# The decay of a gated linear recurrence: from tanh and reciprocal to an exponential on ScalarE

## The chip, the core and the metric

The kernel runs on one core of a Trainium2 chip. A core has TensorE (PE, matrix products; its weight loads are listed as PEld), VectorE (DVE), ScalarE (ACT), GpSimd (POOL) and SyncE (SP), whose queue issues most DMAs. Each engine runs its instructions in the order in which the program wrote them and waits on semaphores for others. The metric is device time in microseconds (us) of one execution, the median of the runs.

## What is computed

One layer of a streaming encoder over 2048 positions of width 1024: a mixer with three parallel branches (A a gated MLP over blocks, B a gated linear recurrence, C a state-space layer), then a two-level mixture of experts, then a norm. The change lies in branch B:

```python
def mixer_rglru(x_raw, g_raw, conv_w, conv_b, rg_w, rg_b, ig_w, ig_b, lam):
    xc = causal_depthwise_conv(x_raw, conv_w, conv_b)
    ...
    r = jax.nn.sigmoid(jnp.einsum("bshi,hij->bshj", xh, rg_w).reshape(bsz, seq, width) + rg_b)
    i = jax.nn.sigmoid(jnp.einsum("bshi,hij->bshj", xh, ig_w).reshape(bsz, seq, width) + ig_b)
    log_a = -LRU_C * r * jax.nn.softplus(-lam)          # LRU_C = 8
    a = jnp.exp(log_a)
    b = jnp.sqrt(-jnp.expm1(2.0 * log_a)) * (i * xc)
    h = linear_recurrence(a, b)                         # h_t = a_t * h_{t-1} + b_t
    return h * jax.nn.gelu(g_raw)
```

## The kernel before, in words

The mixer takes the sequence in two halves of 1024 positions. For each half the input projection `z = x @ W_in` runs in column chunks on TensorE (lines 90 to 92, three matmuls of a split product), and what follows a chunk is a Python generator, put into a list (`Flow`). Each `tick` of that list, called between the matmuls, lets every generator write its instructions up to its next `yield`; `yield 0` hands over within the same tick. A table `TURNS`, keyed by the generator's number and its step, moves single steps. So the order in which each engine gets its instructions is fixed by the steps of all generators, and a generator with a step less stands differently against the others.

Branch B has 12 tiles: two halves, three blocks of 128 channels, two quarters of 512 positions. `b_z` writes the projection of a tile, `b_post` the rest. In `b_post`: the convolution on `xc` (ScalarE line 906, then six VectorE instructions, line 171 as a helper's line, and a copy, line 912); the GELU of the gate (`bgg`, line 916); two gate matmuls (line 922) into two banks of the pool `psm`, which has two; their tanh (line 923) into `tr` (`btr` in the profile) and `ti` (`bti`); then the part that is changed; then the scan (line 939), the product with the gate on GpSimd (`bgg`), a DMA of it, its square (line 946) and a matmul against ones (line 950).

The part that is changed uses T = tanh(-log_a / 2): since a = 2/(1+T) - 1 and sqrt(1 - a^2) = 2 sqrt(T)/(1+T), it takes a tanh and a square root on ScalarE and a reciprocal on VectorE. `b_cols[:, :, 0]` holds the factor of that tanh, made once in `s5_consts`.

`s5_consts` is the setup of branch C; it runs between the tiles 1 to 4 of branch B, in rounds: in each, `angles` builds a table of sines on VectorE, ScalarE and GpSimd, and `outer` (line 691) products on VectorE and GpSimd; a matmul (line 734) into a `psm` bank is read by VectorE into `kp` (line 735), from where a DMA takes it. Later VectorE copies a weight of branch A out of PSUM (`wsT`, line 750). Lines 169, 170 and 171 are the helpers `tt`, `ts` and `stt`, so their instructions are told apart by their tiles. Line 212 and 216 scale the projection's weights on ScalarE; `c_batch` (lines 784 to 829) is branch C's batch with its own matmuls (792, 798, 817 to 819); `part` (lines 997 to 1015) is branch A's.

Of the kernel before, what the change touches and what calls it, by code (L numbers as in the profile page):

```python
# [9 lines left out]
F32 = mybir.dt.float32  # L10
# [3 lines left out]
AF = mybir.ActivationFunctionType  # L14
OP = mybir.AluOpType
# [4 lines left out]
P = 128  # L20
# [124 lines left out]
def phases12(tc, io, hd, hc, tab, gcol, ident, c8, stg):  # L145
# [3 lines left out]
    V, A, G, T = nc.vector, nc.scalar, nc.gpsimd, nc.tensor  # L149
    ctx = ExitStack()  # L150
    with ctx:
# [17 lines left out]
        tt = lambda o, a, b, op, e=V: e.tensor_tensor(out=o, in0=a, in1=b, op=op)  # L169
        ts = lambda o, a, s1, s2, o0, o1=OP.bypass, e=V: e.tensor_scalar(out=o, in0=a, scalar1=s1, scalar2=s2, op0=o0, op1=o1)  # L170
        stt = lambda o, a, s, b, o0, o1: V.scalar_tensor_tensor(out=o, in0=a, scalar=s, in1=b, op0=o0, op1=o1)  # L171
# [215 lines left out]
        b_cols = base.tile([P, 3, 4], F32, name="b_cols")  # L387
# [7 lines left out]
        def s5_consts(pp):  # L395
# [223 lines left out]
            t1, t2, t3 = sm("t1", 3), sm("t2", 3), sm("t3", 3)  # L619
# [21 lines left out]
            tt(t3, t3, t1, OP.add, e=G)  # L641
            yield 0
            ts(sp, t3, 2.0, None, OP.mult)
            yield 0
            ts(b_cols[:, :, 1], col("b_rg_b", 0, 3), 0.5, None, OP.mult)
            pass
# [237 lines left out]
        def b_z(h, i, w, q):  # L884
            N = 512
            F.until(lambda: all(("x", h * 8 + q * 4 + t) in done for t in range(4)) and "bcols" in done)
            st = {}
            for s in range(2):
                ps = bank(psz, "z")
                for k in range(8):  # L890
                    split3(nc, ps, [w[:, j, k, s * P:(s + 1) * P] for j in range(2)],
                           [xT[:, j, k, q * N:(q + 1) * N] for j in range(2)], k == 0, k == 7)
                    if k == 3:
                        F.tick()
                if s == 0:
                    F.add(b_post(h, i, q, ps, st))
                else:
                    st["g"] = ps
                F.tick()

        def b_post(h, i, q, px, st):
            N = 512
            bw = pools["b"]
            cw = lambda k: col("b_conv_w", k * 3 + i)
            xc = bw.tile([P, N], F32, name="bxc", bufs=2)
            A.activation(xc, px, AF.Identity, scale=cw(3), bias=col("b_conv_b", i))
            cst = hst[:, i, 0:3]
            for k in range(3):
                n = 3 - k
                stt(xc[:, n:], px[:, :N - n], cw(k), xc[:, n:], OP.mult, OP.add)  # L910
                stt(xc[:, :n], cst[:, k:3], cw(k), xc[:, :n], OP.mult, OP.add)
            V.tensor_copy(cst, px[:, N - 3:])
            while "g" not in st:
                yield
            gg = bw.tile([P, N], F32, name="bgg", bufs=2)
            A.activation(gg, st["g"], AF.Gelu_apprx_tanh)
            yield
            tr = bw.tile([P, N], F32, name="btr")
            ti = bw.tile([P, N], F32, name="bti")
            for j, o in enumerate((tr, ti)):  # L920
                ps = bank(psm, "m")
                T.matmul(ps, bd[:, j, i, :], xc, start=True, stop=True)
                A.activation(o, ps, AF.Tanh, scale=0.5, bias=b_cols[:, i, 1 + j:2 + j])
            yield

            A.activation(tr, tr, AF.Tanh, scale=b_cols[:, i, 0:1], bias=b_cols[:, i, 0:1])
            stt(ti, ti, 1.0, xc, OP.add, OP.mult)
            sq = bw.tile([P, N], F32, name="bsq")
            A.activation(sq, tr, AF.Sqrt)
            yield  # L930
            ts(tr, tr, 1.0, None, OP.add)
            V.reciprocal(out=tr, in_=tr)  # L932
            yield 0
            tt(sq, sq, tr, OP.mult)
            yield 0
            tt(ti, ti, sq, OP.mult)
            yield 0
            ts(tr, tr, 2.0, -1.0, OP.mult, OP.add)
            V.tensor_tensor_scan(out=xc, data0=tr, data1=ti, initial=hst[:, i, 3:4], op0=OP.mult, op1=OP.add)
            V.tensor_copy(hst[:, i, 3:4], xc[:, N - 1:N])  # L940
            yield
            tt(gg, gg, xc, OP.mult, G)
            yield
            t0 = h * 8 + q * 4
            nc.sync.dma_start(out=yTd[t0:t0 + 4, :, 3 + i, :].rearrange("t p n -> p t n"), in_=gg.rearrange("p (t n) -> p t n", n=P))
            A.activation(xc, gg, AF.Square)
            yield
            ps = bank(psm, "m")
            for t in range(4):
                T.matmul(ps[:, t:t + 1], xc[:, t * P:(t + 1) * P], ones, start=True, stop=True)  # L950
            s_ = ssd[:, 1, t0:t0 + 4]
            tt(s_, s_, ps[:, 0:4], OP.add)
            done.add(("b", h, i, q))
# [427 lines left out]
        open_pool("prep")  # L1381
        F.add(xprep(2))
        F.add(s5_consts(pools["prep"]))

        def pipeline(lst):
# [55 lines left out]
        for h in range(2):  # L1441
            F.until(lambda: ("r", h) in done)
            for m in range(4):
# [4 lines left out]
                for t in range(8):  # L1448
                    F.until(lambda: ("y", h * 8 + t) in done and h * 8 + t in ht)
                    N = 276 if m == 3 else 256  # L1450
# [551 lines left out]
```

## Time and profile before

| | |
|---|---|
| median of 3 runs | 1661.69 us (1660.15 to 1671.78) |
| the profiled execution | 1667.31 us, its span 1665.5 us |
| mean granted TensorE clock | 0.95 |
| TensorE busy | 1510.0 us, 91% of the span |
| VectorE busy | 1028.5 us, 62% |
| ScalarE busy | 915.6 us, 55% |
| GpSimd busy | 693.2 us, 42% |

The span runs from the first to the last instruction; 1.8 us of the execution lie around it. The profiled execution is 5.6 us above the median. Branch B's tiles stand between 95 and 555 us of the span; the experts' first matmul (line 1693) starts at 843.7 us.

### The profile page before, as it was taken

The page shows a single profiled execution, that of the slowest core. Times are in us where ns is not written, and L with a number is a line of the kernel's source. Part 1 is how long each engine was busy: PE and PEld are TensorE (multiplying, and loading weights), DVE is VectorE, ACT ScalarE, POOL GpSimd, SP SyncE. Part 2 cuts the span into 40 slices and gives each one's busy share as a digit, 9 for nine tenths or more (in the row PEclk, how much of TensorE's full clock was granted, in tenths as well). Part 3 has the DMA queues.
Part 4 walks back from the last instruction along what each step waited for, and adds up shares of the span by engine and source line. Part 5 has one row for each costly group of instructions (what it writes and reads, how often), then busy time and mean ns, then how long its engine had stood idle before and what let it go on. Part 6 is the DMA issues. An engine that isn't in the chain of part 4 may idle for free.

```text
span 1665.5 us, 25734 instructions
## 1 busy us (share of the span) xinstructions
PE 1510.0 (91%) x8389; PEld 1295.1 (78%) x8390; DVE 1028.5 (62%) x1813; ACT 915.6 (55%) x2029; POOL 693.2 (42%) x553
## 2 busy tenths in 40 slices
PE   7885689989999999989589969999999999999993
PEld 6763469966788999989578858888888888888882
DVE  6399876367365165777888877578788767403001
ACT  6455345656755556543144635666566656656662
POOL 1286412142202153442144534556555555545442
PEclk8998799999999999999789989999999999999996
DMA  6232572331262352940677878678978876633442
GB/s 165 70 71 60 95 208 78 114 102 51 77 209 64 134 202 77 339 155 37 220 256 228 247 239 243 172 196 261 280 228 244 251 223 195 176 83 96 86 115 79
DMA packets 210063, 267.47 MB, mean 161 GB/s; under 512 B 30600, under 2 KB 174160, under 8 KB 209936
## 3 DMA queue, kind: packets, MB, share of 16 engines
q1 hardware_dynamic: 185456, 203.52, 38.6%
q0 software_dynamic: 24480, 62.27, 15.5%
q8 instruction: 78, 1.28, 0.3%
q14 instruction: 49, 0.40, 0.1%
HBM read 217.09 MB, written 76.94 MB: 177 GB/s over the span
## 4 chain that ended last, share of the span: by engine, by line
PE 61%; DVE 14%; DMA 6%; ACT 3%; issue 2%; POOL 1%; SPq 1%; POOLq 0%; DVEq 0%; ACTq 0%
PE pg L1693 21%; PE z L90 6%; PE z L92 6%; PE z L91 6%; PE pd L1734 4%; PE pd L1733 4%; PE pd L1732 4%; DMA stg<-in_expert_w_up_dram 3%; DVE ring L1601 2%; DVE ring L1619 2%; PE pt L1700 2%; DVE btr L932 1%; PE pt L1705 1%; PE ph L1700 1%; PE m L246 1%
## 5 line engine op out<-in xcount | busy, mean ns | idle before, releaser
L1693 PE MATMUL pg<-ring,xs 128*128 x2016 | 488.2, 395 | 14.1 <-DVE ring L1619 13.0
L1693 PEld LDWEIGHTS pg<-ring,xs 128*128 128x128 f32 x2016 | 378.5, 190 | 94.3 <-issue 16.5
L90 PE MATMUL z<-w,xT 128*128 128x256 f32 (+1 forms) x848 | 252.3, 297 | 17.9 <-ACT xT L302 8.9
L169 POOL TENSOR_TENSOR w<-raw,w 128x512 fp32r<-128x512 f32 x84 | 115.0, 1371 | 348.3 <-ACT raw L216 302.9
L92 PE MATMUL z<-w,xT 128*128 128x256 f32 (+1 forms) x848 | 246.5, 291 | 5.8 <-DVE xT L169 5.7
L91 PE MATMUL z<-w,xT 128*128 128x256 f32 (+1 forms) x848 | 245.9, 290 | 0.0
L1601 DVE TENSOR_SCALAR ring<-stg,gcol 128x512 fp32r<-128x512 f32 x242 | 133.3, 612 | 166.4 <-PE pg L1693 86.7
L1619 DVE SCALAR_TENSOR_TENSOR ring<-stg,gcol,ring 128x512 fp32r<-128x512 f32 x248 | 218.4, 940 | 0.0
L90 PEld LDWEIGHTS z<-w,xT 128*128 128x128 f32 x848 | 166.1, 196 | 21.7 <-issue 10.4
L92 PEld LDWEIGHTS z<-w,xT 128*128 128x128 f32 x848 | 165.6, 195 | 7.2 <-DVE xT L169 7.2
L91 PEld LDWEIGHTS z<-w,xT 128*128 128x128 f32 x848 | 166.2, 196 | 1.7 <-issue 1.7
L1897 POOL DMA_INDIRECT hd<-yb,tab x41 | 75.8, 1848 | 180.5 <-ACT yb L1836 180.5
L1732 PE MATMUL pd<-ring,hh 128*128 x336 | 131.5, 391 | 1.7 <-DVE hh L1638 1.7
L1733 PE MATMUL pd<-ring,hh 128*128 x336 | 131.2, 390 | 0.0
L1734 PE MATMUL pd<-ring,hh 128*128 x336 | 131.2, 390 | 0.0
L1911 POOL TENSOR_TENSOR hs<-hs,hu 128x256 f32<-128x256 f32 x84 | 102.1, 1215 | 54.0 <-ACT hu L1815 51.5
L1946 POOL TENSOR_TENSOR yb<-yb,gf 128x1024 f32<-128x1024 f32 x40 | 117.0, 2924 | 6.8 <-ACT hu L1861 6.8
L171 DVE SCALAR_TENSOR_TENSOR ht<-z,rsd,ht 128x256 f32<-128x256 f32 x176 | 84.7, 483 | 49.8 <-PE z L92 40.3
L90 PE MATMUL z<-xT,w 128*128 128x512 f32 x256 | 113.4, 443 | 0.2 <-ACT xT L302 0.2
L212 ACT ACTIVATE w<-raw,vec 128x256 fp32r<-128x256 f32 x176 | 86.6, 495 | 48.1 <-PE z L92 47.2
L91 PE MATMUL z<-xT,w 128*128 128x512 f32 x256 | 103.6, 405 | 0.2 <-DVE xT L169 0.2
L92 PE MATMUL z<-xT,w 128*128 128x512 f32 x256 | 103.1, 403 | 0.0
(443 smaller groups left out, 2862.0 us busy)
## 6 DMA issues: line engine op xcount, KB each, us to landing
stg<-in_expert_w_gate_dram SPq DMA_DIRECT2D x62, 512.0 KB
stg<-in_expert_w_up_dram SPq DMA_DIRECT2D x62, 512.0 KB
stg<-in_expert_w_down_dram SPq DMA_DIRECT2D x60, 512.0 KB
raw<-in_w_in_dram SPq DMA_DIRECT2D x48, 256.0 KB
raw<-in_w_out_dram SPq DMA_DIRECT2D x24, 512.0 KB
ht<-in_x_dram SPq DMA_DIRECT2D x16, 512.0 KB
yp<-yTd SPq DMA_DIRECT2D x8, 1024.0 KB
hd<-ht SPq DMA_DIRECT2D x16, 512.0 KB
```

What stands on the lines that cost most here:

```text
L90: nc.tensor.matmul(ps, ah, bh, start=first, stop=False)
L91: nc.tensor.matmul(ps, ah, bl, start=False, stop=False)
L92: nc.tensor.matmul(ps, al, bh, start=False, stop=last)
L169: tt = lambda o, a, b, op, e=V: e.tensor_tensor(out=o, in0=a, in1=b, op=op)
L1601: x = v.tensor_scalar(out=ring[:, r, 0, sl], in0=src[:, sl], scalar1=g, scalar2=None, op0=OP.mult)
L1619: x = v.scalar_tensor_tensor(out=ring[:, r, 1, sl], in0=src[:, sl], scalar=g, in1=hi, op0=OP.mult, op1=OP.subtract)
L1693: i = t.matmul(pg[f], xx[j // 2], w[j % 2], start=k == 0 and j == 0, stop=k == 7 and j == 2)
L1732: t.matmul(pd[n], hh[:, 0, kf], w[0], start=kf == 0, stop=False)
L1733: t.matmul(pd[n], hh[:, 0, kf], w[1], start=False, stop=False)
L1734: i = t.matmul(pd[n], hh[:, 1, kf], w[0], start=False, stop=kf == 3)
L1911: g.tensor_tensor(out=o, in0=o, in1=hu[:, f * 256:(f + 1) * 256], op=OP.mult).then_inc(s_hm, 1)
L1946: g.tensor_tensor(out=z, in0=z, in1=gf, op=OP.mult).then_inc(p_z, 1)
```

## The change

The decay a is taken directly: its logarithm is log_a = -4 softplus(-lam) (1 + t), where t is the tanh of the gate that `tr` holds, so one `Exp` with a scale and a bias per channel gives it (`b_cols[:, :, 3]`, made once). T stays, for the square root: sqrt(1 - a^2) / 2 = (1 + a) sqrt(T/4). The reciprocal and the three VectorE instructions around it go; one instruction with two operations comes.

```diff
@@ s5_consts
             ts(sp, t3, 2.0, None, OP.mult)
+            ts(b_cols[:, :, 3], t3, -4.0, None, OP.mult)
             yield 0
@@ b_post
-            A.activation(tr, tr, AF.Tanh, scale=b_cols[:, i, 0:1], bias=b_cols[:, i, 0:1])
+            sq = bw.tile([P, N], F32, name="bsq")
+            A.activation(sq, tr, AF.Tanh, scale=b_cols[:, i, 0:1], bias=b_cols[:, i, 0:1])
             stt(ti, ti, 1.0, xc, OP.add, OP.mult)
-            sq = bw.tile([P, N], F32, name="bsq")
-            A.activation(sq, tr, AF.Sqrt)
-            yield
-            ts(tr, tr, 1.0, None, OP.add)
-            V.reciprocal(out=tr, in_=tr)
-            yield 0
-            tt(sq, sq, tr, OP.mult)
+            A.activation(tr, tr, AF.Exp, scale=b_cols[:, i, 3:4], bias=b_cols[:, i, 3:4])
+            A.activation(sq, sq, AF.Sqrt, scale=0.25)
+            yield
+            stt(sq, tr, 1.0, sq, OP.add, OP.mult)
             yield 0
             tt(ti, ti, sq, OP.mult)
             yield 0
-            ts(tr, tr, 2.0, -1.0, OP.mult, OP.add)
             V.tensor_tensor_scan(out=xc, data0=tr, data1=ti, initial=hst[:, i, 3:4], op0=OP.mult, op1=OP.add)
```

Behind the change the lines of `b_post` before the scan shift by up to two. VectorE's order in the first tile's changed part, from the copy that ends the second tile's convolution (`hst` keeps a tile's last values; a row is line, operation, output<-inputs and size; the scan of line 939 is listed as SCALAR_TENSOR_TENSOR), before:

```order
L912 COPY hst<-z 128x3
L170 TENSOR_SCALAR btr<-btr 128x512
L932 RECIPROCAL btr<-btr 128x512
L169 TENSOR_TENSOR bsq<-bsq,btr 128x512
L169 TENSOR_TENSOR bti<-bti,bsq 128x512
L170 TENSOR_SCALAR btr<-btr 128x512
L939 SCALAR_TENSOR_TENSOR bxc<-btr,hst,bti 128x512
L940 COPY hst<-bxc 128x1
L735 COPY kp<-tp 16x4x128
```

and with the change:

```order
L913 COPY hst<-z 128x3
L171 SCALAR_TENSOR_TENSOR bsq<-btr,bsq 128x512
L169 TENSOR_TENSOR bti<-bti,bsq 128x512
L937 SCALAR_TENSOR_TENSOR bxc<-btr,hst,bti 128x512
L938 COPY hst<-bxc 128x1
L736 COPY kp<-tp 16x4x128
```

Four instructions ahead of the scan have become one, and the copy `kp` stands right behind as before. ScalarE's order in the fourth tile, before:

```order
L793 ACTIVATE cx<-tp 128x256
L926 ACTIVATE btr<-btr,b_cols 128x512
L929 ACT_TABLE_LOAD
L929 ACTIVATE bsq<-btr 128x512
L906 ACTIVATE bxc<-z,vec 128x512
L212 ACTIVATE w<-raw,vec 128x256
```

and with the change:

```order
L794 ACTIVATE cx<-tp 128x256
L928 ACTIVATE bsq<-btr,b_cols 128x512
L930 ACT_TABLE_LOAD
L930 ACTIVATE btr<-btr,b_cols 128x512
L931 ACT_TABLE_LOAD
L931 ACTIVATE bsq<-bsq 128x512
L907 ACTIVATE bxc<-z,vec 128x512
L212 ACTIVATE w<-raw,vec 128x256
```

The exponential and a table load of its own stand between the tanh and the square root's load, and so ahead of the next tile's convolution `bxc`. This is so in all 12 tiles: 34 table loads become 46, and no load at another place comes or goes. ScalarE's order behind the seventh tile's square root, before:

```order
L916 ACT_TABLE_LOAD
L916 ACTIVATE bgg<-z 128x512
L946 ACTIVATE bxc<-bgg 128x512
L923 ACTIVATE btr<-m,b_cols 128x512
L923 ACTIVATE bti<-m,b_cols 128x512
L1011 ACTIVATE uv<-tp 128x4x128 x2
```

and with the change:

```order
L917 ACT_TABLE_LOAD
L917 ACTIVATE bgg<-z 128x512
L924 ACTIVATE btr<-m,b_cols 128x512
L924 ACTIVATE bti<-m,b_cols 128x512
L944 ACTIVATE bxc<-bgg 128x512
L1009 ACTIVATE uv<-tp 128x4x128 x2
```

The square of the gated output (946, now 944) has gone behind the two tanh of the eighth tile. Besides, in two places GpSimd's product `bgg` stands one or two of its weight products earlier, TensorE's matmul against ones (950) of one tile of the second half stands 52 instructions earlier, and VectorE's instructions of a tile stand closer together where others lay between them.

## Rows read from the trace of the kernel before

**Rows 1.** The page's part 1: busy time of each engine, its share of the span and its number of instructions.

```profile
PE 1510.0 (91%) x8389; PEld 1295.1 (78%) x8390; DVE 1028.5 (62%) x1813; ACT 915.6 (55%) x2029; POOL 693.2 (42%) x553
```

**Rows 2.** Busy time of each engine in five stretches of the first third (columns: the stretch in us, its length, busy us of PE, PEld, DVE, ACT and POOL with their instructions, granted TensorE clock, DMA share, GB/s).

```profile
100.00:203.00 103.00, 62.79 (x254) 43.58 (x253) 100.81 (x109) 46.67 (x72) 69.39 (x54) 0.82 0.41 84
203.00:240.00 37.00, 30.12 (x143) 23.43 (x142) 23.84 (x49) 16.45 (x30) 7.61 (x8) 0.87 0.67 169
240.00:340.00 100.00, 97.51 (x714) 90.40 (x713) 53.06 (x126) 58.31 (x136) 15.04 (x17) 0.97 0.39 124
340.00:430.00 90.00, 78.08 (x351) 59.66 (x350) 62.11 (x106) 61.63 (x139) 29.41 (x23) 0.95 0.24 71
430.00:560.00 130.00, 128.21 (x829) 113.48 (x828) 64.57 (x128) 73.44 (x158) 25.63 (x21) 0.97 0.38 116
```

**Rows 3.** The instructions on tiles `btr` and `bti`, over the whole span (line, engine, operation, names, count: shortest/median/longest ns, first and last start in us, form).

```profile
L170 DVE TENSOR_SCALAR btr<-btr x24: 414/419/1700, 133.0 to 536.3; 128x512 f32<-128x512 f32 x24
L926 ACT ACTIVATE btr<-btr,b_cols x12: 801/806/842, 115.2 to 525.4; 128x512 f32<-128x512 f32 x12
L929 ACT ACTIVATE bsq<-btr x12: 629/632/636, 117.3 to 527.5; 128x512 f32<-128x512 f32 x12
L932 DVE RECIPROCAL btr<-btr x12: 3353/3353/3355, 133.4 to 531.6; 128x512 f32<-128x512 f32 x12
L169 DVE TENSOR_TENSOR bsq<-bsq,btr x12: 679/692/753, 136.8 to 534.9; 128x512 f32<-128x512 f32 x12
...
L171 DVE SCALAR_TENSOR_TENSOR bti<-bti,bxc x12: 681/684/1577, 128.5 to 515.9; 128x512 f32<-128x512 f32 x12
```

**Rows 4.** The groups of ScalarE by shape: the table loads charged to line 929 (count, busy us, mean ns, idle us before them).

```profile
L929 ACT ACT_TABLE_LOAD x12 | 15.4, 1283 | 0.2
```

**Rows 5.** VectorE in order of time, three stretches (start us, us, engine, line, operation, names, form, count).

```profile
132.98 0.42 DVE L170 TENSOR_SCALAR btr<-btr 128x512 f32<-128x512 f32 x1
...
138.68 1.28 DVE L939 TENSOR_TENSOR_SCAN bxc<-btr,hst,bti 128x512 f32<-128x512 f32 x1
...
140.08 0.68 DVE L735 COPY kp<-tp 16x512 f32<-16x512 f32 x1
...
164.97 1.70 DVE L170 TENSOR_SCALAR btr<-btr 128x512 f32<-128x512 f32 x1
...
171.88 1.28 DVE L939 TENSOR_TENSOR_SCAN bxc<-btr,hst,bti 128x512 f32<-128x512 f32 x1
...
194.41 0.42 DVE L170 TENSOR_SCALAR btr<-btr 128x512 f32<-128x512 f32 x1
...
200.04 1.28 DVE L939 TENSOR_TENSOR_SCAN bxc<-btr,hst,bti 128x512 f32<-128x512 f32 x1
```

**Rows 6.** TensorE in order of time, the second gate matmul (L922) of the tiles 2, 3 and 4, with the idle time before it and what ended it in brackets.

```profile
140.81 2.08 PE L922 MATMUL m<-bxc,bd 128*128 128x512 f32 x2 [6.70 <-DVE kp L735]
...
174.02 2.08 PE L922 MATMUL m<-bxc,bd 128*128 128x512 f32 x2 [6.96 <-DVE kp L735]
...
202.17 2.08 PE L922 MATMUL m<-bxc,bd 128*128 128x512 f32 x2 [6.63 <-DVE kp L735]
```

**Rows 7.** ScalarE in order of time: the square root of the second tile.

```profile
147.52 0.64 ACT L929 ACTIVATE bsq<-btr 128x512 f32<-128x512 f32 x1
```

**Rows 8.** ScalarE and then VectorE in order of time around the fourth tile.

```profile
212.38 0.80 ACT L926 ACTIVATE btr<-btr,b_cols 128x512 f32<-128x512 f32 x1
...
215.03 0.76 ACT L906 ACTIVATE bxc<-z,vec 128x512 f32<-128x512 f32 x1
...
215.82 0.75 DVE L171 SCALAR_TENSOR_TENSOR bxc<-z,vec,bxc 128x509 f32<-128x509 f32 x1 [6.19 <-ACT bxc L906]
...
219.15 1.01 DVE L750 COPY wsT<-tp 128x384 f32<-128x384 f32 x2
```

**Rows 9.** TensorE in order of time: three of its gaps after the setup.

```profile
219.76 0.69 PE L792 MATMUL tp<-ident,zk 128*128 128x128 f32 x2 [0.81 <-DVE wsT L750]
...
232.48 1.12 PE L922 MATMUL m<-bxc,bd 128*128 128x512 f32 x2 [0.93 <-DVE cv L169]
...
287.01 1.05 PE L950 MATMUL m<-ones,bxc 128*128 128x1 f32 x8 [0.88 <-ACT raw L242]
```

**Rows 10.** ScalarE in order of time around 280 us.

```profile
279.64 0.38 ACT L967 ACTIVATE uv<-z 128x256 f32<-128x256 f32 x1 [3.87 <-DVE tab L170]
...
285.14 0.63 ACT L946 ACTIVATE bxc<-bgg 128x512 f32<-128x512 f32 x1 [0.85 <-POOL bgg L169]
```

**Rows 11.** TensorE in order of time, second half of the sequence: the gate matmuls of tile 9, and two gaps.

```profile
397.41 1.88 PE L922 MATMUL m<-bxc,bd 128*128 128x512 f32 x4
...
403.76 1.96 PE L997 MATMUL m<-uv,wsT 128*128 128x512 f32 x4 [1.68 <-ACT btr L923]
...
423.89 1.56 PE L239 MATMUL tp<-ident,raw 128*128 128x128 f32 x8 [2.06 <-ACT btr L923]
```

**Rows 12.** ScalarE in order of time in the same stretch.

```profile
402.93 0.69 ACT L923 ACTIVATE btr<-m,b_cols 128x512 f32<-128x512 f32 x1 [4.62 <-DVE bxc L939]
...
407.45 0.81 ACT L926 ACTIVATE btr<-btr,b_cols 128x512 f32<-128x512 f32 x1
...
423.15 0.68 ACT L923 ACTIVATE btr<-m,b_cols 128x512 f32<-128x512 f32 x1
```

**Rows 13.** TensorE in order of time: its last gap in the recurrent branch's stretch.

```profile
544.55 4.13 PE L879 MATMUL m<-ones,yc 128*128 128x1 f32 x30 [0.57 <-ACT yc L874]
```

## The prediction, made before the changed kernel ran

> **What bounds the kernel now.** I read the page's busy times first. TensorE is busy 91% of the span [rows 1], so a microsecond saved elsewhere is worth one only where TensorE waits for it. The second view is the table of stretches, read for the busy time of each engine against the length of the stretch. From 100 to 203 us VectorE is busy 100.8 of 103 us and TensorE 62.8: there VectorE is the bound. From 240 to 340 and from 430 to 560 us TensorE has 97.5 of 100 and 128.2 of 130. Between 340 and 430 us it has 78.1 of 90, and ScalarE and VectorE are both near 62 [rows 2]. The third view is TensorE in order of time with the reason for each gap. In the setup each round has a gap of 6.6 to 7.0 us in front of the second gate matmul, released by the copy `kp` on VectorE [rows 6]: that matmul needs the PSUM bank that `kp` empties, and `kp` stands in VectorE's queue behind the previous tile's reciprocal and scan [rows 5]. So the setup's end is a chain on VectorE through the changed instructions of tiles 1, 2 and 3.
>
> **What the change does to VectorE.** Per tile four instructions go: two `ts` of 0.42, the reciprocal of 3.35 and the product of 0.69 us, together 4.88. One `stt` comes; the nearest row is the same form on `bti`, 0.68 us at the median and 1.58 at the worst [rows 3]. Net 4.2 us less per tile (3.3 at worst), 50 us in 12 tiles.
>
> **What it does to ScalarE.** An `Exp` over 128x512 with a scale and a bias per channel is in no row. Below it lies the square root without such operands, 0.63, above it the longest tanh with them, 0.84; I take that tanh's median, 0.81, since shape and operands are the same [rows 3]. The added table load is 1.28 us with next to no idle time around it (0.2 us in all twelve) [rows 4]. Together 2.1 us per tile, 25 us in 12 tiles (1.9 to 2.15). One small instruction for `b_cols` in the setup counts as nothing against this.
>
> A rule of the Trainium skill speaks against this change. On the row, a load costs 1.28 us with no idle time to speak of [rows 4]. "ScalarE: Activation LUTs", section "What ACT_TABLE_LOAD costs", has 1283 ns for the load, which the trace confirms, and another 1380 ns of drain at every switch, which it does not show. By that price each tile would pay 3.5 us on ScalarE, and the sum below would be about 2.8 us smaller.
>
> **A, the setup: 13.0 us less.** From the first removed instruction to the start of the scan VectorE takes 138.68 - 132.98 = 5.70, 171.88 - 164.97 = 6.91 and 200.04 - 194.41 = 5.63 us [rows 5]. With the change 0.68 + 0.69 of work and small steps between remain, 1.48. That leaves 4.2, 5.4 and 4.15, or 13.8 in all; the second includes a `ts` that took 1.70 instead of 0.42, a stall that the new instruction may meet in its place, so 12.5 is the other end. I take 13.0. The longer ScalarE chain does not come into the way: tile 2's root starts at 147.52 and VectorE wants it at 164.97 [rows 5, 7], 17 us of cover against 2.1. What is late next after each saved piece is the rest of VectorE's round: it is busy 98% of the stretch, and GpSimd with 69.4 us and TensorE with 62.8 still fit into 90 [rows 2]. After the third round the DMAs that `kp` feeds, and behind them branch C, simply start earlier, and TensorE follows as a whole.
>
> **B, the fourth tile: 1.7 us more.** Here ScalarE's chain has no cover. Its tanh starts at 212.38, the next convolution's first step at 215.03, and VectorE, idle for 6.19 us, starts on that at 215.82. Behind the convolution it copies `wsT` at 219.15 [rows 8], and TensorE waits 0.81 us for that at 219.76 [rows 9]. With `Exp` and a load in between, all of this moves by 2.1 us, and TensorE has no slack to hide it. Queued behind are branch C's transposes and batches. Some of it comes back: at 232.48 TensorE waits 0.93 us for a bank that VectorE empties behind tile 4's scan; that chain is 4.2 shorter, so only the product itself remains of that wait, about 0.4 returns. Net +1.7 (0 to 2.1).
>
> **C, near 287 us: 0.9 less.** TensorE's 0.88 us wait [rows 9] is for a square on ScalarE at 285.14, behind GpSimd's product. That hangs on ScalarE's weight scaling, which stands behind an evacuation that waited 3.87 us for VectorE at 279.64, where tile 6's chain was in front of it [rows 10]. With 4.2 us less there it closes.
>
> **D, tiles 7 to 10: 2.6 less.** At 402.93 ScalarE has waited 4.62 us for tile 8's scan, and runs from there without a pause to 423.15, where TensorE waits for it (gaps of 1.68 and 2.06 us) [rows 11, 12]. With the change the scan is done before TensorE's gate matmuls, which begin at 397.41 and take 1.88 us; moved up by the 0.7 us that tile 7 gives back, they let ScalarE start at about 398.2, 4.7 us earlier. Inside the run lies tile 9's chain (its tanh at 407.45) with 2.1 us more. So ScalarE reaches the point at 423.15 some 2.6 us earlier, and TensorE with it. It still waits there: ScalarE keeps half of what VectorE gave. The swap of the square and the two tanh in tile 8 only helps here.
>
> **E, at 544 us: 0.6 less.** TensorE's last gap, 0.57 us [rows 13], is for a square behind products that VectorE begins after tile 12's scan; that ends 4 us earlier. The other tiles (5, 6, 11) lie beside a TensorE that is nearly always busy and count as nothing; what hides the 2.1 us there are projection results waiting in four PSUM banks. Without that cover each would cost at most 2.1. The moved `bgg` products and the earlier matmul against ones find their inputs ready, and count as nothing.
>
> **The sum** is -13.0 + 1.7 - 0.9 - 2.6 - 0.6 = -15.4 us. The experts behind 560 us keep their order and their durations, so they start earlier as a block. The profiled execution took 1667.3 us and would take 1651.9. It stands 5.6 us above the median, and nothing in it says where; the runs shown spread from 1660.15 to 1671.78. From the median of 1661.7 the forecast is **1646.3 us**.
>
> **Rivals.**
> 1. *More than that.* After gaps of 6.6 to 7.0 us TensorE starts slowly: two gate passes take 2.08 us [rows 6], where four take 1.88 at 397.41 [rows 11], and the granted clock is 0.82 and 0.87 in the first two stretches [rows 2], between the levels of 1.2 and 2.4 GHz. The gaps shrink to about 2.6, and the clock may stay up. In the setup that changes nothing, since VectorE is the bound; from 203 to 240 us 30.1 us of TensorE work at 0.87 could become 26.2, 3.9 less. With A at 13.8 the time is 1641.6. Against it: another wait for a DMA falls into that stretch.
> 2. *ScalarE pays more at a switch.* If each added switch costs its load's 1.28 us [rows 4] once again, in waiting, a tile has 3.4 us more in place of 2.1: B grows by 1.3, D shrinks by 1.3, and the time is 1648.9. The 0.2 us of idle time before twelve loads speak against it. The drain in the Trainium skill's "ScalarE: Activation LUTs" is such a cost.
> 3. *The setup does not shrink.* GpSimd works in step with VectorE there; if half of each saving turns into a wait for its products, A is 6.5 and the time 1652.8. GpSimd's 67% of that stretch [rows 2] speaks against it.
> 4. *Slower.* ScalarE's convolution step stands behind the new load in every tile, and VectorE and TensorE behind it, as in B. Were all 12 tiles like the fourth, without the gain of A, the price would be 12 x 2.1 = 25 us and the time 1686.8. It decides where ScalarE's chain has less than 2.1 us of cover; the setup's tiles have 17 [rows 5, 7].
> 5. *The change does not do what it says*: the order shows that all 12 reciprocals go, and that each tile gets one load more, no other; this I count at nothing.
>
> **How the numbers follow.** Forecast 0.60, rival 1 0.18, rival 2 0.08, rival 3 0.10, rival 4 0.04. One per cent, 16.6 us, is about what a measurement of this kernel can tell from no change: under 1645.1 is faster. The forecast's own spread, from the ends of A, B and `Exp`, is some 4 us to each side; a third of its chance lies below the line, 0.20, and rival 1 nearly whole, 0.17: faster 0.37. Slower is rival 4, 0.04. The rest, 0.59, is within 1%. The range for 8 in 10 goes from below rival 1 by half the forecast's own spread to above rival 3 by as much, since the median itself moves by a few microseconds: 1639 to 1655.
>
> **What would show it.** In the profile of the changed kernel: VectorE about 50 us less busy, ScalarE 25 more, 46 table loads; the gaps in front of `kp`'s matmul down from 6.6 to 7.0 us to 1.5 to 2.7; the third setup round's scan ending 13 us earlier, at about 188; TensorE's gap before the transpose near 207 (219.76 before) up from 0.8 to 2.9; a wait for ScalarE's gate tanh still there near 409. The forecast is wrong if the setup's rounds do not get shorter, or if TensorE shows new waits for ScalarE between 230 and 330 or behind 420 us.

## The result and the profile after

The changed kernel takes 1644.33 us (median of 4 runs, 1638.97 to 1648.28), the kernel before beside it 1662.65 us: a ratio of 0.988 (95% interval 0.983 to 0.993), 18.3 us less by the medians. The ratios here and below are not quotients of the two medians and can differ from them by up to 0.002. Repeated beside two other series it took 1643.49 (0.990, 0.988 to 0.993) and 1647.88 us (0.991, 0.989 to 0.993). The forecast was 1646.3. The profiled execution of the changed kernel took 1643.64 us, its span 1641.9.

Busy time of each engine, part 1 of the page of the changed kernel, to be held against [rows 1]:

```profile
PE 1508.7 (92%) x8389; PEld 1294.2 (79%) x8390; DVE 976.0 (59%) x1778; ACT 942.4 (57%) x2053; POOL 692.8 (42%) x553
```

VectorE has lost 52.5 us and ScalarE gained 26.8 (forecast 50 and 25); TensorE's work is the same. Of the 52.5 us the time got less than 20.

VectorE in the setup's three rounds, changed kernel, in order of time (the instruction that replaced the reciprocal, the scan, and in the first round the copy `kp`):

```profile
134.45 0.68 DVE L171 SCALAR_TENSOR_TENSOR bsq<-btr,bsq 128x512 f32<-128x512 f32 x1
...
135.96 1.28 DVE L937 TENSOR_TENSOR_SCAN bxc<-btr,hst,bti 128x512 f32<-128x512 f32 x1
...
137.36 0.68 DVE L736 COPY kp<-tp 16x512 f32<-16x512 f32 x1
...
162.28 1.97 DVE L171 SCALAR_TENSOR_TENSOR bsq<-btr,bsq 128x512 f32<-128x512 f32 x1
...
165.01 1.28 DVE L937 TENSOR_TENSOR_SCAN bxc<-btr,hst,bti 128x512 f32<-128x512 f32 x1
...
187.52 0.68 DVE L171 SCALAR_TENSOR_TENSOR bsq<-btr,bsq 128x512 f32<-128x512 f32 x1
...
188.96 1.28 DVE L937 TENSOR_TENSOR_SCAN bxc<-btr,hst,bti 128x512 f32<-128x512 f32 x1
```

From the first instruction of the changed part to the scan the three rounds took 5.70, 6.91 and 5.63 us [rows 5]; now 1.51, 2.73 and 1.44. That is 12.6 less in all.

TensorE's gaps in the changed kernel (idle time and its releaser in brackets), to be held against [rows 6, 9, 11]:

```profile
138.09 2.08 PE L923 MATMUL m<-bxc,bd 128*128 128x512 f32 x2 [1.56 <-DVE kp L736]
...
167.14 2.07 PE L923 MATMUL m<-bxc,bd 128*128 128x512 f32 x2 [2.78 <-DVE kp L736]
...
191.09 2.07 PE L923 MATMUL m<-bxc,bd 128*128 128x512 f32 x2 [1.52 <-DVE kp L736]
...
204.24 0.55 PE L750 MATMUL tp<-ident,big 128*128 128x128 f32 x3 [3.76 <-DMA big<-in_a_spatial_w_dram]
...
210.75 0.69 PE L793 MATMUL tp<-ident,zk 128*128 128x128 f32 x2 [2.32 <-DVE wsT L751]
...
249.83 1.10 PE L923 MATMUL m<-bxc,bd 128*128 128x512 f32 x2 [1.28 <-DVE cv L169]
...
409.14 1.72 PE L239 MATMUL tp<-ident,raw 128*128 128x128 f32 x8 [2.97 <-ACT btr L924]
...
473.65 1.16 PE L799 MATMUL m<-cx,cpp 128*128 128x128 f32 x8 [1.39 <-ACT raw L242]
```

In front of the matmul that waits for `kp` 6.6 to 7.0 us [rows 6] are down to 1.5 to 2.8 (1.5 to 3.3 in the two repeats). The gap for `wsT` is 2.32 where it was 0.81 [rows 9]; the other two gaps of [rows 9] are gone, as are the 1.68 us at 403.76 [rows 11] and the last one [rows 13]. A wait for ScalarE's gate tanh near 409 stays (2.97 for 2.06). One wait for VectorE, 1.28 us at 249.83 in front of tile 6's gate matmuls, and one for ScalarE, 1.39 us at 473.65, are new; a new wait for ScalarE behind 420 us is one of the signs by which the prediction was to be wrong.

ScalarE in the fourth tile, changed kernel (against [rows 8]), and the two groups of table loads of the changed part over the whole span:

```profile
201.27 0.80 ACT L928 ACTIVATE bsq<-btr,b_cols 128x512 f32<-128x512 f32 x1
202.09 1.28 ACT L930 ACT_TABLE_LOAD   x1
203.38 0.81 ACT L930 ACTIVATE btr<-btr,b_cols 128x512 f32<-128x512 f32 x1
204.20 1.28 ACT L931 ACT_TABLE_LOAD   x1
205.50 0.63 ACT L931 ACTIVATE bsq<-bsq 128x512 f32<-128x512 f32 x1
206.03 0.76 ACT L907 ACTIVATE bxc<-z,vec 128x512 f32<-128x512 f32 x1
```

```profile
L930 ACT ACT_TABLE_LOAD x12 | 15.4, 1283 | 0.2
L931 ACT ACT_TABLE_LOAD x12 | 15.4, 1283 | 0.1
```

From the tanh's start to the convolution's it is 4.76 us, where it was 215.03 - 212.38 = 2.65 [rows 8]: 2.11 more. Of that the exponential is 0.81 and the load 1.28, and what follows a load starts 0.01 to 0.02 us behind it.

### The profile page after: what moved, and what is told of

It reads as the page before. It is cut to its first block, busy times and chain, and to the rows that moved or that the text cites. A ratio compares the mean times of both kernels' runs of the same rounds, so it can differ in the third digit from the quotient of the medians.

```text
span 1641.9 us, 25729 instructions
## 1 busy us (share of the span) xinstructions
PE 1508.7 (92%) x8389; PEld 1294.2 (79%) x8390; DVE 976.0 (59%) x1778; ACT 942.4 (57%) x2053; POOL 692.8 (42%) x553
## 3 DMA queue, kind: packets, MB, share of 16 engines
q0 software_dynamic: 24480, 62.27, 15.6%
q8 instruction: 78, 1.28, 0.3%
## 4 chain that ended last, share of the span: by engine, by line
PE 64%; DVE 12%; DMA 5%; ACT 4%; issue 2%; POOL 1%; SPq 0%; POOLq 0%; DVEq 0%; ACTq 0%
PE pg L1691 22%; PE z L90 7%; PE z L91 6%; PE z L92 6%; PE pd L1732 4%; PE pd L1730 4%; PE pd L1731 4%; DMA stg<-in_expert_w_up_dram 3%; DVE ring L1599 2%; DVE ring L1617 2%; PE pt L1698 2%; PE pt L1703 1%; DVE bxc L171 1%; PE ph L1698 1%; PE m L863 1%
## 5 line engine op out<-in xcount | busy, mean ns | idle before, releaser
L1599 DVE TENSOR_SCALAR ring<-stg,gcol 128x512 fp32r<-128x512 f32 x242 | 143.8, 655 | 169.9 <-PE pg L1691 87.6
L1617 DVE SCALAR_TENSOR_TENSOR ring<-stg,gcol,ring 128x512 fp32r<-128x512 f32 x248 | 203.1, 879 | 0.0
```

The lines of the kernel that those rows point to most:

```text
L1599: x = v.tensor_scalar(out=ring[:, r, 0, sl], in0=src[:, sl], scalar1=g, scalar2=None, op0=OP.mult)
L1617: x = v.scalar_tensor_tensor(out=ring[:, r, 1, sl], in0=src[:, sl], scalar=g, in1=hi, op0=OP.mult, op1=OP.subtract)
```

## The experiments

One table for all. Each entry is how much earlier than in the profile of the kernel before an instruction starts, in us, read from each trace: the third tile's scan (200.04 there), the first, fourth, seventh and eighth group of matmuls that read `rw` (line 246; 291.06, 431.67, 527.43, 571.16), and the first expert matmul (843.68). Differences of neighbouring columns say what a stretch gave or took.

| kernel | scan 3 | 291 | 432 | 527 | 571 | experts | median us |
|---|---|---|---|---|---|---|---|
| before, again | -1.0 | -3.6 | -0.2 | 0.4 | 2.0 | 3.3 | 1659.9 |
| changed | 11.1 | 12.0 | 14.7 | 13.9 | 17.0 | 18.3 | 1644.3 |
| changed, again | 11.1 | 12.1 | 17.0 | 15.7 | 18.8 | 19.0 | 1643.5 |
| changed, third | 12.0 | 12.9 | 15.3 | 14.1 | 15.6 | 15.5 | 1647.9 |
| setup only | 11.3 | 9.8 | 9.8 | 9.7 | 9.8 | 9.8 | 1647.4 |
| rest only | -3.4 | -3.2 | 0.3 | -0.9 | 2.1 | 2.0 | 1659.0 |
| no exponential | 13.9 | 18.8 | 27.0 | 27.5 | 30.5 | 32.1 | (1569.4) |
| exponential added to before | -1.6 | -7.9 | -7.1 | -9.0 | -9.9 | -9.8 | 1670.9 |
| exponential later | 12.4 | 17.7 | 22.6 | 21.5 | 23.0 | 22.4 | 1640.2 |
| exponential later, again | 11.9 | 17.6 | 20.1 | 18.9 | 20.4 | 20.2 | 1640.3 |
| `uv` on VectorE | 12.6 | 13.1 | 18.5 | 17.7 | 19.2 | 17.5 | 1641.0 |
| later, `uv` on VectorE in half 1 | 12.3 | 17.2 | 22.8 | 20.8 | 22.3 | 22.6 | 1640.1 |

### The kernels repeated

> The kernel before once more, unchanged, for a second profile. Between the first profile of before (span 1665.5) and that of the change (span 1641.9) 23.6 us lie, of which 18.3 are there when the experts' first matmul starts (843.7 against 825.4 us) and 5.2 come in the experts' stretch, which the change does not touch. Theory (the 5.2 us are spread between executions, waits for expert weights): the stretch from the experts' first matmul to the end, 821.8 us in the first profile of before, is nearer to the 816.5 of the change here, by 2 us or more, and the span is about 1660. Rival (the change shortens the experts): it is 821 to 822 again.

> The full change once more, for a second profile beside those of this call and more times: 1644 to 1648, a ratio to before of 0.989 to 0.991; the experts' stretch, 816.5 us in its first profile, within 3 us of that; the lead of tile 3's scan over the kernel before 11 to 12 us, of the start of the experts 15 to 18.

> The changed kernel as it is, in five rounds beside the two versions with the exponential later. 1642 to 1645 us, as in its first two runs; TensorE 1.3 to 2.5 us late for `wsT` near 210 us.

The second profile of before (span 1658.2) puts a scale on every comparison: it is 7.3 us shorter than the first with the same code. Between the third scan and 291 us it falls 2.6 us behind the first, and has made that up again by the second group that reads `rw`, near 333 us. The start of the experts spreads from 840.4 to 843.7 before and from 824.7 to 828.2 after. The means of these starts, 842.0 and 826.1, are 15.9 us apart. The first pair of profiles differs by 23.6 us in span, of which 5.3 lie behind that start; from there to the end the two profiles of before take 821.8 and 817.8 us, the changed kernel 816.5 and, repeated, 814.4 and 818.5. Each kernel spreads there by 4 us, so those 5.3 us cannot be put down to the change. The third series of the changed kernel is slower than I expected from the first two. Differences in the table of under 2 to 3 us say nothing on their own.

One stretch is free of this spread: from the first changed instruction of tile 1 to the third scan VectorE takes 67.06 and 67.10 us in the two profiles of before, and 54.50 to 54.51 in the three of the changed kernel. What differs is where this chain starts, 132.98 and 133.94 us before, 133.50 to 134.47 after, so part of each entry under "scan 3" stands ahead of the change.

### The setup's three tiles alone, and all others alone

> The change in tiles 1 to 3 alone; the other nine tiles keep tanh, square root and reciprocal. Theory (term A of the prediction): 12.5 to 13.8 us less than before, so about 1649.5, and the gaps in front of the gate matmul that waits for kp down to 1.5 to 2.8 us. Rival 3 (the setup is held by something else): 6.5 us less. If the tiles 4 to 12 bring as much as the first profiles say (5 to 6 us beyond A), this kernel stays above the full change by that.

> The change in tiles 4 to 12 alone; tiles 1 to 3 keep the reciprocal. Theory (terms B to E): +1.7 - 0.9 - 2.6 - 0.6 = -2.4 us, and up to 3.3 us more where the first profile of the change shows a higher granted clock after the small matmuls near 530 us and shorter waits near 700 us: -2.4 to -5.7, 1657 to 1660. Rival 4 (ScalarE's longer chain is what TensorE waits for): slower than before, up to +19 for nine tiles.

```diff
+if h == 0 and 2 * i + q < 3:     # setup only; the other run has the opposite
     (the new lines)
+else:
+    (the old lines)
```

The setup alone: 1647.35 us, 0.990 (0.988 to 0.992), 14.5 less than the 1661.84 beside it. TensorE's lead of 11.3 us at the third scan falls to 9.8 at 291 and stays there to the experts: once won it is carried through unchanged. The rest alone: 1658.97 us, 0.998 (0.996 to 0.9995), 2.9 less. The parts add up to 17.4 us. So the setup's chain carries most of the gain, and in nine of twelve tiles 38 us taken off VectorE bought 2.9 us (0.8 to 6.5 by the interval). The split is good to a few us: the one profile of the setup alone, an execution 3.4 us above the median, starts the experts 9.8 us earlier than the first profile of before and 6.5 earlier than the second; the chain itself is 12.6 us shorter there too (54.50 us).

### ScalarE's part taken out, and put alone into the kernel before

> The change without its exponential (the decay is left out: the gate's tanh stands in its place, so the recurrence is another one), thus without the added table load: VectorE's part of the change alone. Theory: A 13.0, B turned to -0.4, C 0.9, D 4.7 and E 0.6, together -19.6 us from before, plus what the clock gives; 3 to 5 us below the full change, about 1640. Rival 4 (ScalarE's 2.1 us are paid in all 12 tiles): 25 us below the full change, about 1619. Third possibility (ScalarE's part costs nothing anywhere): the same as the full change.

```diff
-A.activation(tr, tr, AF.Exp, scale=b_cols[:, i, 3:4], bias=b_cols[:, i, 3:4])
```

Without the exponential the scan gets the gate tanh as its decay. The experts then get other blocks, so it is compared only up to where they start. At 527 us TensorE is 27.5 us ahead of before, 13.6 more than with the exponential in the first profile (11.8 and 13.4 more than in the repeats). Of that, 2.8 us (2.8 and 1.8) are there at the third scan, and they are not the exponential's: from the first changed instruction of tile 1 to that scan VectorE takes 54.50 us, as with the exponential, but this chain starts at 131.67 us here, and TensorE's transposes near 103 us, ahead of any exponential, are already 1.8 us earlier. In the setup the 17 us of cover hide the exponential whole. So of the 25 us that ScalarE pays in twelve tiles 9 to 12 reach the point at 527; I had counted the fourth tile and tiles 7 to 10, some 4 us.

Up to 291 us the price is 3.9 to 4.1 us. TensorE's trace has it at the wait for `wsT` (2.32 us with the exponential, none at that place without), at matmuls behind this wait (granted clock 0.76 from 211 to 219 us, against 0.87 in the same work without), and at the 1.28 us of 249.83, which stand behind tile 5's chain and are gone without the exponential. From there to 432 us it is 5.4 us (3.3 and 5.8 against the repeats), and up to 527 another 1.3 to 1.8, tile 11's wait.

TensorE's gap near 400 us in that run, to be held against 409.14 in the changed kernel; there is no gap for `wsT` and none near 470:

```profile
400.08 1.09 PE L239 MATMUL tp<-ident,raw 128*128 128x128 f32 x8 [1.33 <-ACT btr L924]
```

The gap is 1.6 us shorter, and that is not all of the price there. TensorE in the 8 us up to this gap's end and the 8 us behind it (length, busy us, granted clock, DMA share, GB/s), in the changed kernel:

```profile
401.00:409.00 8.00, 4.75 (x16) 1.00 0.13 49
409.00:417.00 8.00, 7.86 (x30) 0.57 0.56 152
```

without the exponential:

```profile
392.00:400.00 8.00, 6.75 (x26) 1.00 0.13 46
400.00:408.00 8.00, 7.92 (x51) 1.00 0.58 158
```

and in the kernel before, behind its gap of 2.06 us [rows 11]:

```profile
424.00:432.00 8.00, 8.00 (x32) 0.57 0.53 145
```

Behind the longer waits TensorE spends most of 8 us at its lower level of 1.2 GHz (0.60 and 0.58 in the repeats of the changed kernel, 0.57 in the second profile of before); behind the wait of 1.33 us it stays at 2.4 GHz. By these rows that is worth 3.4 us, more than the wait itself. What makes the clock fall behind one wait and not behind the other is not shown.

> The kernel before with ScalarE's part of the change alone: between tanh and square root an exponential with the same operands writes a tile that the root then overwrites, so 12 exponentials and 12 table loads more; the reciprocal stays. Every engine's order is as before otherwise. Theory: the setup hides it (17 us of cover); B +2.1, tiles 8 and 9 in D +2.1 each, the others 0 to 1: 5 to 8 us slower than before, about 1668. The run without the exponential, where TensorE ran 13.5 us ahead of the full change by 527 us, says that ScalarE's part costs more once VectorE's is shorter; it needs no more here, where VectorE's chain is still long. Rival 4 (paid in every tile): +25, 1687. Rival 2 (a switch costs more than its load): 3.4 per paying tile, 9 to 13 us slower.

```diff
 A.activation(tr, tr, AF.Tanh, scale=b_cols[:, i, 0:1], bias=b_cols[:, i, 0:1])
 sq = bw.tile([P, N], F32, name="bsq")
+A.activation(sq, tr, AF.Exp, scale=b_cols[:, i, 3:4], bias=b_cols[:, i, 3:4])
 A.activation(sq, tr, AF.Sqrt)
```

1670.85 us, 1.006 (1.003 to 1.009), 9.3 us slower than the 1661.55 beside it. By its time this fits rival 2, by its rows it does not. ScalarE in the fourth tile of this run:

```profile
215.12 0.80 ACT L927 ACTIVATE btr<-btr,b_cols 128x512 f32<-128x512 f32 x1
215.94 1.28 ACT L930 ACT_TABLE_LOAD   x1
217.23 0.81 ACT L930 ACTIVATE bsq<-btr,b_cols 128x512 f32<-128x512 f32 x1
218.06 1.28 ACT L931 ACT_TABLE_LOAD   x1
219.36 0.63 ACT L931 ACTIVATE bsq<-btr 128x512 f32<-128x512 f32 x1
219.89 0.76 ACT L907 ACTIVATE bxc<-z,vec 128x512 f32<-128x512 f32 x1
```

From tanh to convolution it is 4.77 us, 2.12 more than before [rows 8]: the price of a tile is the 2.1 of the forecast, and no waiting is added at the switch. What was too small is the number of tiles that pay. In the setup nothing is added (67.06 us from tile 1's first changed instruction to the third scan, as before). Against the second profile of before the lag grows by 3.8 us from the third scan to 291, by 2.7 from there to 432, and by 2.4 more up to 527; against the first it is 6.3, -0.7 and 1.8. Three of TensorE's gaps in this run show places where it pays:

```profile
224.60 0.69 PE L793 MATMUL tp<-ident,zk 128*128 128x128 f32 x2 [2.65 <-DVE wsT L751]
...
411.95 1.96 PE L999 MATMUL m<-uv,wsT 128*128 128x512 f32 x4 [3.10 <-ACT btr L924]
...
496.21 1.16 PE L799 MATMUL m<-cx,cpp 128*128 128x128 f32 x8 [1.40 <-ACT raw L242]
```

They are the gap for `wsT` (0.81 before [rows 9]), the one for the gate tanh (1.68 before [rows 11]) and that of tile 11, which the changed kernel has at 473.65 and neither the kernel before nor the one without the exponential has.

### The exponential one step later

> The full change with one yield 0 in front of the exponential: the next tile's convolution on ScalarE goes ahead of the exponential, both loads and the root, in tiles 1 to 5, 8 and 11. Theory (term B: TensorE's 2.3 us in front of the transpose behind wsT hang on that convolution): this gap back to 0.8 or less, and 1.5 to 2 us faster than the full change. Other theory (B is given back a few us later anyway, at TensorE's waits near 220 us): the gap closes, the time stays within 1 us of the full change.

> The later exponential alone again, beside the other two on one chip. My theory: 1638 to 1642 us, 2 to 4 us below the changed kernel, since it starts the experts 3.4 us earlier and nothing behind that differs. If the 3 us of its first run are the spread between executions, it is within 1 us of the changed kernel.

```diff
+yield 0
 A.activation(tr, tr, AF.Exp, scale=b_cols[:, i, 3:4], bias=b_cols[:, i, 3:4])
```

The next tile's convolution then stands ahead of the exponential and both loads on ScalarE. 1640.19 us (0.989, 0.986 to 0.992) and 1640.33 us (0.987, 0.985 to 0.989), each time faster by the median than the changed kernel beside it, by 3.3 and 7.5 us, where I had expected 1.5 to 2 and then 2 to 4. The first pair's intervals overlap; the second pair's do not (0.9891 against 0.9893), with the changed kernel at its slowest there. TensorE in the first of the two around the fourth tile:

```profile
205.98 2.05 PE L799 MATMUL m<-cx,cpp 128*128 128x128 f32 x8 [1.26 <-DVE wsT L751]
```

The gap at line 793 (2.32 above) is gone. A smaller wait for `wsT` stands earlier, and nothing over 0.3 us follows up to 300. From the third scan to 291 us the lead grows by 5.3 and 5.7 us, where the changed kernel's grows by 0.9 to 1.1. The work on ScalarE is the same; its place in ScalarE's queue, ahead of the convolution that VectorE and TensorE hang on, cost over 4 us, as much as the exponential's whole price in this stretch. The wait for the gate tanh (2.98 and 3.02 us) and tile 11's (1.39) stay as they were. By its medians this version is faster than both kernels, and none of those below is clearly faster still.

### The evacuations of branch A on VectorE

> The full change with branch A's 12 evacuations of line 1009 moved from ScalarE to VectorE; six stand in the stretch of tiles 8 to 10. Theory (term D: there ScalarE is what TensorE waits for, 2.97 us near 409, and VectorE has room since the change): 3.2 us off ScalarE's run, the wait down to under 1, 2.5 to 3 us faster than the full change. If TensorE's wait there has another cause: no change.

```diff
-A.activation(uv[c][:, th * 4:th * 4 + 4, 1, :], pp_[th], AF.Copy)
+V.tensor_copy(uv[c][:, th * 4:th * 4 + 4, 1, :], pp_[th])
```

1640.99 us (0.988, 0.986 to 0.990), 2.5 less than the changed kernel beside it, with intervals that overlap. The wait for the gate tanh shrinks by 0.6, where under 1 us was to be left of it:

```profile
406.95 1.09 PE L239 MATMUL tp<-ident,raw 128*128 128x128 f32 x8 [2.36 <-ACT btr L924]
```

Behind it the granted clock is 0.79 over 8 us, against 0.57 to 0.60 with the changed kernel. Behind 571 us, where the second half's evacuations stand among VectorE's work for the router, 1.7 of the 19.2 us are lost again; the changed kernel's own profiles move between -0.1 and +1.3 there, so that these copies cost it is likely and not shown.

> The changed kernel with the exponential issued one step later (the next tile's convolution ahead of it) and, in the first half alone, the evacuations of the branch A transposes (line 1009) on VectorE. My theory, from the two runs that made these edits apart: the first keeps the wait for `wsT` near 210 us closed (2.3 us) and the second gains some 2.5 us more between 370 and 430 us, without the 2 us that the second half's evacuations lost between 600 and 690 us. So TensorE is 22 to 26 us ahead of the kernel before at 527 us, the experts start at 819 to 822 us, and the time is 1636 to 1640 us. If the two edits draw on the same idle time, the experts start no earlier than with the later exponential alone (821.3 us) and the time is 1639 to 1643 us.

```diff
+if h == 0:
+    V.tensor_copy(uv[c][:, th * 4:th * 4 + 4, 1, :], pp_[th])
+else:
     A.activation(uv[c][:, th * 4:th * 4 + 4, 1, :], pp_[th], AF.Copy)
```

1640.11 us (0.987, 0.986 to 0.989), with the experts at 821.1 us: no better than the later exponential alone. With both edits the gap reads

```profile
402.68 1.09 PE L239 MATMUL tp<-ident,raw 128*128 128x128 f32 x8 [2.85 <-ACT btr L924]
```

against 2.98 and 3.02 us with the later exponential alone. My sum of the two gains was wrong. The wait at the gate tanh is hardly shortened by taking the 1.1 us of copies away; what shortened it was the exponential's absence (1.33). Which of ScalarE's instructions there could move was not tried.

## Why the prediction held, and where its steps did not

**The bound.** VectorE's chain bounded the setup, as read from [rows 2, 5, 6]; the setup alone gave 14.5 us by the medians, and the gaps for `kp` shrank as foreseen.

**A** was forecast at 13.0 and measured 12.6 by the instructions of the chain, in every profile. By the third scan's start it is 11.1 to 13.0 (188.0 to 189.0, against 200.04 in one profile of before and 201.04 in the other), since the chain starts at different times ahead of the change. The small excess is the middle value that I took for round 2: the long `ts` there, 1.70 us, did meet the new instruction, which took 1.97 instead of 0.68, so the lower end, 12.5, was right.

**B** was the step that failed, in two of its terms. The wait for `wsT` came as forecast: 2.32 us with the exponential, none at that place without it or with it later, near the 2.1 (against the first profile of before it grew by 1.5). But the exponential's whole price up to 291 us was 4, since tile 5, counted at nothing in E, pays too (1.28 us at 249.83), and the matmuls behind the wait run at a lower granted clock. And VectorE's shorter chain gave back more: without the exponential the lead grows by 4.9 us in this stretch against the first profile of before and by 7.5 against the second, where B and C together had 1.3. **C**, the gap at 287, closed as foreseen. B and C together were forecast 0.8 us slower; the three profiles show 0.9 to 1.1 us faster against the first profile of before and 3.4 to 3.6 against the second, two errors of 2 to 6 us that in part cancel.

**D** came out at 2.7, 3.1 and 2.8 us (the starts of the third and fourth group that reads `rw`), forecast 2.6, with the wait for the gate tanh left near 409 as foreseen; the second profile of before has the same length here as the first. The working was too small on both sides here as well: VectorE's part alone gives 8.3 us between the same two points (run without the exponential; forecast 4.7), and the exponential takes 5.2 to 5.6 of that (forecast 2.1). In both the same term is missing, the 3.4 us that the lower clock behind the long wait costs: without it the two are about 4.9 and 2, as in the prediction. The working left it out on both sides, and since the kernel before and the changed one both pay it, it cancels. (The 0.7 us of tile 7 in this term stand in no row; the trace of before has them as a gap of 0.68 us at 388.26, which the changed kernel lacks.)

**E** was forecast at 0.6. Tile 11's new wait takes 0.8 to 1.3 us up to 527. The prediction had named a new wait for ScalarE behind 420 us as a sign that it is wrong, and what it got wrong is the cover that E gave to the tiles 5, 6 and 11: two of the three pay. From 527 to 571 the three profiles gain 3.1, 3.1 and 1.5 us; the gap is 0.57 of that, and the rest goes with the granted clock, below. In sum 0.3 to 2.3 us against the first profile of before; against the second it is -1.8 to 0.2, so nothing can be said of E but that its gap closed.

**The sum**, 15.4 us less, stands against 18.3, 18.1 and 14.1 by the medians of the three series, and against 15.9 by the start of the experts. It is right, and the setup, the bulk of it, for the reason given. Beyond the setup the agreement is luck: I had less than half of what VectorE gives (6.0 of 13.6 us up to 527) and less than half of what ScalarE takes (4.2 of 9 to 12), and the two errors cancel. To a time within 1% of the kernel before I gave a chance of 0.59, to a faster one 0.37; by the medians the three series are 1.1, 1.1 and 0.8% faster, on that line.

**The rivals.** 1, the clock: TensorE's stretch behind the setup, here with that before it, shows

```profile
100.00:190.00 90.00, 64.85 (x256) 44.59 (x254) 88.26 (x97) 52.60 (x77) 66.61 (x53) 0.83 0.47 96
190.00:227.00 37.00, 29.10 (x128) 22.50 (x129) 21.47 (x48) 18.39 (x31) 9.24 (x9) 0.80 0.67 170
```

a granted clock of 0.80, below the 0.87 of [rows 2], not above (0.77 and 0.81 in the repeats; the second profile of before has 0.78 in the stretch of [rows 2]). The wait for a DMA at 204.24, 3.76 us, stands in it, as one of 3.38 does before; whether it is the cause is not shown. VectorE still fills 88.3 of 90 us of the setup. 2, a dearer switch: each switch costs its load and no more. The Trainium skill, "ScalarE: Activation LUTs", section "What ACT_TABLE_LOAD costs", gives 1283 ns, which all 24 loads above show, and 1380 ns of drain, of which the rows show 0.01 to 0.02 us; a sum by that price, an estimate, would be 2.8 us smaller and no nearer. 3, a setup that does not shrink: refuted by the setup alone. 4, a ScalarE without cover in all tiles: the exponential alone cost 9.3 us of the 25, so something over a third of the way, and nothing in the setup's tiles. 5: the change did what it says (34 table loads became 46, 12 of them in front of the exponential).

## What to carry to other kernels

Work moved from the engine that bounds a stretch pays in that stretch in full (12.6 us off the chain of 3 tiles, 14.5 us off the time of 1661.8), and elsewhere only by the difference between what one engine gives and the other takes, so both have to be sized tile by tile, as runs that make one half of the change alone do. A busy TensorE around a tile does not make added ScalarE work free: 9 to 12 us of 25 came through, or 9.3 where VectorE's part was left as it was. A wait of TensorE can cost more than its length: behind one of 2.97 us came 3.4 us of matmuls at the lower clock, behind one of 1.33 none. Where a moved operation lands in the new engine's queue counts too: one `yield 0`, which let the next tile's first step go ahead of it, gave 3.3 and 7.5 us more, where the whole change gave 2.9 in nine tiles.

## What was unexpected

**The long instruction in round 2.** It stays where it is, whatever stands there: a `ts` of 1.70 to 1.71 us in all four profiles that keep the reciprocal there (0.42 in the other tiles), and the new `stt` at 1.96 to 1.97 us in all nine that do not (0.68 in nearly all other tiles). GpSimd runs a memory fill of 0.46, a copy of 0.18 and a product of 1.04 us beside it in both. That these are its cause is likely, but was not tested.

**The clock behind the last gap.** TensorE's windows of 10 us (length, busy us, granted clock, DMA share, GB/s) in the first profile of before:

```profile
540.00:550.00 10.00, 9.43 (x64) 0.86 0.43 131
550.00:560.00 10.00, 10.00 (x67) 0.80 0.15 54
```

and in the changed kernel, 13 us earlier in the sequence:

```profile
530.00:540.00 10.00, 10.00 (x72) 0.83 0.30 92
540.00:550.00 10.00, 10.00 (x81) 1.00 0.17 61
```

After the gap of 0.57 us and 30 matmuls of 128x1 [rows 13] TensorE ran on at a granted clock of 0.80, so partly at its lower level of 1.2 GHz, while the changed kernel, which runs the same small matmuls from 528.85 us without a gap, was back at 2.4 GHz after one such window. The gap is not the cause, as two more profiles show. The second one of before has the same gap and 0.96 in its next window,

```profile
550.00:560.00 10.00, 10.00 (x79) 0.96 0.21 54
```

and gains 1.6 us there over the first. The third one of the changed kernel has no gap and the lowest clock of all:

```profile
530.00:540.00 10.00, 10.00 (x59) 0.66 0.26 67
```

So the clock falls at the small matmuls with the gap and without it, and by these windows costs 1.7 to 3.4 us in either kernel. That is the spread of this stretch between executions, and not a gain of the change. What decides its size stays open.
